# The rotation of the next head's queries: all of it on VectorE, and ahead of both softmax divisions

## The chip, the cores and the metric

One Trainium2 chip, one core of it. The metric is the device time of one execution in microseconds. The engines are called as in the profile: PE (TensorE), DVE (VectorE), ACT (ScalarE), POOL (GpSimd), SP (SyncE, which here issues the DMAs).

## What is computed

One layer of a diffusion backbone over 512 latent and 256 context tokens of width 2048: a modulated RMSNorm, one input projection, then eight heads of gated DeltaNet and eight heads of attention side by side, SiLU gates on both, one output projection and a final RMSNorm. The change lies in the attention heads. There each query head is RMS-normalised, scaled by a weight and rotated by a 2-D axial rotary table, and then meets 768 keys:

```python
def apply_rope(x, cos, sin):
    B, L, H, _ = x.shape
    xr = x.astype(jnp.float32).reshape(B, L, H, 2, 2, ROPE_HALF)
    x1, x2 = xr[..., 0, :], xr[..., 1, :]
    c = cos[None, :, None]
    s = sin[None, :, None]
    out = jnp.stack([x1 * c - x2 * s, x2 * c + x1 * s], axis=-2)
    return out.reshape(B, L, H, HEAD_DIM).astype(x.dtype)
...
def attend(q_blk, k_all, v_all):
    s = jnp.einsum('bqkgd,bskd->bkgqs', q_blk, k_all).astype(jnp.float32) * (HEAD_DIM ** -0.5)
    p = jax.nn.softmax(s, axis=-1).astype(v_all.dtype)
    return jnp.einsum('bkgqs,bskd->bqkgd', p, v_all)
```

## The kernel before, in words

The kernel runs in stages: modulation and norm of the tokens, projections with the DeltaNet scan (up to about 936 us of the span), attention (936 to about 1213 us), output projection with the final norm. Each product is made of three fp32r matmuls from a high and a low half of its operands, so most results are split: ACT writes the rounded high half (L122, L815) and another engine subtracts it to get the low half.

The attention stage is a loop over 17 steps, `for u in range(2 * NH + 1)` (L1266). Step u works on head h = u // 2 and on half qp = u % 2 of its 512 queries (two blocks of 128). Inside this stage the order of the instructions on PE, ACT, DVE and POOL is the order in which the code writes them; each engine runs its own list in that order and waits for what an instruction needs. Four strands are woven together in one step:

- The scores of this step: three matmuls for each part of 128x768 scores into one PSUM tile `s` (`attn_scores`, L1103), the row maxima on DVE (L1114, L1115), the exponentials with their row sums on ACT (L1119, tile `pr`), and for both blocks a reciprocal and a division on DVE (`attn_over`, L1123 to L1125). `pr` holds 128x768 fp32.
- The step before: its divided `pr` blocks are transposed on PE (tile `pt`, L1133), in three groups of 8, split into `pth` on ACT and `ptl` on DVE (L815, L816), and multiplied with the values (tile `o`, `attn_values`, L1140). Two groups of transposes stand at the head of the step ahead of the scores, the third after the first run of filler.
- The filler: the gate projection's matmuls (`fillers`, tile `zl`, L1197), 12 groups of three per step, placed by `fill(n)`: 4 after the scores, 4 before the values, 1 and 3 around the next head's queries. Their weights come by DMA, are split on ACT (L122) and POOL (`wlo_z`, L123). When a projection ends, `z_over` (L1155) puts a tanh on ACT and two operations on DVE (L212, L1161). Every second group also calls for one row of a gate vector: a DMA (`graw`), a scaling on ACT (L1236) and an addition on POOL (`gacc`, L1238).
- The queries of the next head, in odd steps with a head to follow (u = 1, 3, ..., 13, seven of them; they are numbered 1 to 7 here). The generator `attn_norm` (L1075) runs in pieces. Its first piece, in the step before, transposes the raw queries and takes the row sums. The second, called by `next(qns)` after the scores, multiplies by the row's scale on DVE (L1087, the profile gives the helper's line L215: `qn<-qn,hss`) and forms the swapped product on POOL (L1090, `rt<-qn,tabq`; the profile leaves out digits in names, the tile is `rt2`). `swapped` reads each pair of 32 columns in exchanged order. The third piece multiplies by the cosine table (`qn<-qn,tabq`) and adds `rt2` (L1094), both on DVE. It is called between the two calls of `attn_over`. Later in the step `attn_qt` (L1097) transposes the rotated queries on PE (tile `qtp`, L820), and splits them into `qTh` on ACT and `qTl` on DVE (L815, L816). The next step's scores read both.

The transposes of `pt` and `qtp` take turns in two PSUM buffers (tag `t`, `bufs=2`): the second group of `pt` transposes of an even step takes the buffer that `qtp` held until `qTl` was written.

In an odd step the list of DVE after the exponentials is: `ptl` of the third group, reciprocal and division of block 0, the two operations of the rotation, reciprocal and division of block 1, what `z_over` and the values ask for, `qTl`.

Of the kernel before, what the change touches and what calls it, by code (L numbers as in the profile page):

```python
# [68 lines left out]
def build(tc, a):  # L69
    nc = tc.nc  # L70
    V, S, G, T, SY = nc.vector, nc.scalar, nc.gpsimd, nc.tensor, nc.sync
# [134 lines left out]
    def power(x, p):  # L206

        n = x.shape[-1]
        G.tensor_tensor(out=x, in0=x, in1=expo[p][:, :n], op=ALU.pow)

    def silu(eng, out, x, t):
        eng.scalar_tensor_tensor(out=out, in0=t, scalar=1.0, in1=x, op0=ALU.add, op1=ALU.mult)  # L212

    def mul(eng, out, x, y):
        eng.tensor_tensor(out=out, in0=x, in1=y, op=ALU.mult)  # L215
# [570 lines left out]
    def swapped(x):  # L786

        return x.rearrange("p t (a s r) -> p (t a) s r", a=2, s=2)[:, :, ::-1]
# [29 lines left out]
    def transposes(src, t0, n, tp):  # L818
        for t in range(n):
            T.transpose(out=tp[:, t], in_=src[:, (t0 + t) * 128:(t0 + t + 1) * 128], identity=ident)  # L820
        return tp
# [243 lines left out]
    def ttile(shape, nm):  # L1065
        return PSt.tile(shape, F32, tag="t", bufs=2, name=nm)
# [3 lines left out]
    def attn_q(h):  # L1070
        qc = ap_.tile([128, SEQ], F32, tag="qc", bufs=2, name=f"qc{h}")
        SY.dma_start(qc, qad[h])
        return qc

    def attn_norm(h, qc):  # L1075

        tp = transposes(qc, 0, 4, ttile([128, 4, 128], f"qtp{h}"))
        qn = ap_.tile([128, 4, 128], F32, tag="qn", bufs=1, name=f"qn{h}")
        ss = ap_.tile([128, 4], F32, tag="hss", bufs=2, name=f"hss{h}")
        jk = ap_.tile([128, 128], mybir.dt.bfloat16, tag="hjk", bufs=1, name=f"hjk{h}")  # L1080
        S.copy(qn, tp)
        for t in range(4):
            S.activation(jk, qn[:, t], AF.Square, accum_out=ss[:, t:t + 1])
        V.tensor_scalar(out=ss, in0=ss, scalar1=1.0 / 128.0, scalar2=EPS, op0=ALU.mult, op1=ALU.add)
        power(ss, -0.5)
        yield qn
        mul(V, qn, qn, ss.unsqueeze(2).to_broadcast([128, 4, 128]))  # L1087
        t2 = ap_.tile([128, 4, 128], F32, tag="rt2", bufs=1, name=f"rt2{h}")
        tb = A["tab"]
        mul(G, t2.rearrange("p t (a s r) -> p (t a) s r", a=2, s=2), swapped(qn),  # L1090
            tb[:, 1].rearrange("p t (a s r) -> p (t a) s r", a=2, s=2))
        yield qn
        mul(V, qn, qn, tb[:, 0])
        V.tensor_tensor(out=qn, in0=qn, in1=t2, op=ALU.add)  # L1094
        yield qn

    def attn_qt(h, qn):  # L1097
        tp = transposes(qn.rearrange("p t d -> p (t d)"), 0, 4, ttile([128, 4, 128], f"qtp2{h}"))
        qt = [apr.tile([128, SEQ], F32R, tag=i, bufs=2, name=f"{i}{h}") for i in ("qTh", "qTl")]
        split_from(tp.rearrange("p t c -> p (t c)"), *qt)  # L1100
        return qt

    def attn_scores(h, qp, qTh, qTl):  # L1103

        kv = h // 4
        sp = PSs.tile([128, 2 * NTOK], F32, tag="s", name=f"s{h}_{qp}")
        sos = [sp[:, qi * NTOK:(qi + 1) * NTOK] for qi in range(2)]
        mxs = [ap_.tile([128, 2], F32, tag="mx", bufs=4, name=f"mx{h}_{qp}_{qi}") for qi in range(2)]
        for qi in range(2):
            qsl = slice((qp * 2 + qi) * 128, (qp * 2 + qi + 1) * 128)  # L1110
            for c0, c1 in (((0, 512), (512, 768)) if qi == 0 else ((0, 256), (256, 768))):
                mm3(sos[qi][:, c0:c1], qTh[:, qsl], qTl[:, qsl], kTh[:, kv, c0:c1], kTl[:, kv, c0:c1], True, True)
        for qi in range(2):
            V.tensor_reduce(out=mxs[qi][:, 0:1], in_=sos[qi], axis=AX.X, op=ALU.max)  # L1114
            V.tensor_scalar(out=mxs[qi][:, 0:1], in0=mxs[qi][:, 0:1], scalar1=-SC, scalar2=None, op0=ALU.mult)  # L1115
        prs = []
        for qi in range(2):
            pr = ap_.tile([128, NTOK], F32, tag="pr", bufs=4, name=f"pr{h}_{qp}_{qi}")
            S.activation(pr, sos[qi], AF.Exp, bias=mxs[qi][:, 0:1], scale=SC, accum_out=mxs[qi][:, 1:2])  # L1119
            prs.append(pr)  # L1120
        return list(zip(prs, mxs))

    def attn_over(pr, mx):  # L1123
        V.reciprocal(mx[:, 1:2], mx[:, 1:2])
        V.tensor_scalar(out=pr, in0=pr, scalar1=mx[:, 1:2], scalar2=None, op0=ALU.mult)  # L1125

    def attn_pt(h, qp, prs, j2):

        tp3 = ttile([128, 2, 256], f"pt{h}_{qp}_{j2}")
        for qi in range(2):  # L1130
            for jj in range(2):
                j = j2 * 2 + jj
                T.transpose(out=tp3[:, jj, qi * 128:qi * 128 + 128],  # L1133
                            in_=prs[qi][0][:, j * 128:j * 128 + 128], identity=ident)
        pth = ap_.tile([128, 2, 256], F32R, tag="pth", bufs=3, name=f"pth{h}_{qp}_{j2}")
        ptl = ap_.tile([128, 2, 256], F32R, tag="ptl", bufs=3, name=f"ptl{h}_{qp}_{j2}")
        split_from(tp3, pth, ptl)
        return pth, ptl

    def attn_values(h, qp, pts):  # L1140
        kv = h // 4
        op = PSt.tile([128, 256], F32, tag="o", name=f"o{h}_{qp}")
        for j in range(6):
            vsl = slice(kv * 128, kv * 128 + 128)
            mm3(op, vah[:, j, vsl], val[:, j, vsl], pts[j // 2][0][:, j % 2], pts[j // 2][1][:, j % 2], j == 0, j == 5)
        m = M[8 + h][:, qp * 256:qp * 256 + 256]
        if (h, qp) in early:
            V.scalar_tensor_tensor(out=m, in0=m, scalar=0.5, in1=op, op0=ALU.mult, op1=ALU.mult)
        else:
            S.copy(m, op)  # L1150
        done.add((h, qp))
# [107 lines left out]
    def fill(n):  # L1259

        for _ in range(n):
            next(gen, None)
# [3 lines left out]
    for u in range(2 * NH + 1):  # L1266
        h, qp = divmod(u, 2)
        more = h + 1 < NH
        prs, pts = None, []
        if before is not None:  # L1270
            pts = [attn_pt(*before, j2) for j2 in range(2)]
        if h < NH:
            prs = attn_scores(h, qp, *qt)
            if qp == 1 and more:
                next(qns)
            fill(FS + 5 * (before is None))
        if before is not None:
            pts.append(attn_pt(*before, 2))
        if prs is not None:
            attn_over(*prs[0])  # L1280
            if qp == 1 and more:
                qn = next(qns)
            attn_over(*prs[1])
        if before is not None:
            fill(FV)
            attn_values(before[0], before[1], pts)
        if u < NZA:

            e = ap_.tile([128, SEQ], F32, tag="ze", bufs=2, name=f"zae{u}")
            S.activation(e, M[8 + u], AF.Tanh, scale=0.5)  # L1290
            silu(V, M[8 + u], M[8 + u], e)
            early.update(((u, 0), (u, 1)))
        fill(FQ)
        if more:
            if qp == 0:
                qns = attn_norm(h + 1, qcs.pop(h + 1))
                next(qns)
                if h + 3 < NH:
                    qcs[h + 3] = attn_q(h + 3)
            else:  # L1300
                qt = attn_qt(h + 1, qn)
        fill(FR)
        before = h, qp, prs
# [109 lines left out]
```

## Time and profile before

Three runs took 1404.99, 1405.37 and 1408.50 us; the median is 1405.37. The profile was taken from a further execution.

| | |
|---|---|
| time of the profiled execution | 1413.92 us |
| its span, first to last instruction | 1412.1 us |
| PE busy (matmuls) | 1282.5 us, 91% |
| DVE busy | 747.5 us, 53% |
| ACT busy | 608.3 us, 43% |
| POOL busy | 529.4 us, 37% |
| mean granted clock of PE | 0.975 of full speed |

How to read it: busy time is the union of an engine's recorded instructions, and its share is of the whole span, over stages with different limits. A timeline row has the start, the duration, the engine, the line, the operation with its tiles as out<-in, the shape and the count, and in square brackets the idle time of the engine in front of it and what ended that. The granted clock has two levels, full (2.4 GHz, written 1.0) and half (1.2 GHz, 0.5); a mean between them is a stretch with some of each.

### The profile page before, as it was taken

How to read it: one execution, taken by the hardware profiler on the slowest of the kernel's cores; microseconds unless marked ns; L12 is line 12 of the kernel's file. 1: busy time of each engine (PE TensorE's matmuls, PEld its weight loads, DVE VectorE, ACT ScalarE, POOL GpSimd, SP SyncE). 2: the span in 40 equal slices, each digit the busy share in tenths (PEclk: the TensorE clock that was granted, in tenths of full speed). 3: DMA queues.
4: the chain of work that ended last, by engine and by line, in shares of the span. 5: the costliest groups of instructions: out<-in, count | busy, mean ns of one | idle time of the engine just before them, and what ended most of it. 6: DMA issues, size and time to landing. Idle time of an engine off the chain costs nothing.

```text
span 1412.1 us, 24988 instructions
## 1 busy us (share of the span) xinstructions
PE 1282.5 (91%) x9406; PEld 1031.0 (73%) x9406; DVE 747.5 (53%) x1643; ACT 608.3 (43%) x1509; POOL 529.4 (37%) x477
## 2 busy tenths in 40 slices
PE   3788988999999999999999999889889999999997
PEld 1455676877788787787777877667777778787785
DVE  3434685475456656476665524427566655544322
ACT  4111342445444453544545444446556663433221
POOL 1011211334353453443434445435777772012330
PEclk9999998999999999999999999999999999999999
DMA  9999622222322223232232343353545432474202
GB/s 311 255 270 285 180 72 56 71 56 63 67 71 69 66 65 77 58 84 57 81 66 58 84 127 111 93 186 105 145 132 151 134 97 61 164 234 146 90 33 102
DMA packets 264187, 163.52 MB, mean 116 GB/s; under 512 B 63042, under 2 KB 236187, under 8 KB 263043
## 3 DMA queue, kind: packets, MB, share of 16 engines
q1 hardware_dynamic: 264067, 161.93, 41.6%
q8 instruction: 74, 1.21, 0.4%
q14 instruction: 46, 0.38, 0.1%
HBM read 148.33 MB, written 13.56 MB: 115 GB/s over the span
## 4 chain that ended last, share of the span: by engine, by line
PE 55%; DVE 17%; DMA 8%; issue 8%; ACT 7%; POOL 4%; SPq 2%; POOLq 0%; ACTq 0%; DVEq 0%
PE zl L1197 6%; PE vl L157 5%; DMA wada<-in_w_ada 4%; PE kl L157 3%; PE vx L159 3%; DVE cacc_k L199 2%; DVE cacc_v L199 2%; PE kvl L157 2%; PE po L140 2%; PE tsh L751 2%; PE po L141 2%; PE po L139 2%; PE ql L157 2%; PE kx L159 2%; PE tsh L740 2%
## 5 line engine op out<-in xcount | busy, mean ns | idle before, releaser
L215 POOL TENSOR_TENSOR sdh<-sth,egl 128x256 f32<-128x256 f32 x80 | 55.4, 692 | 169.5 <-DVE sth L757 75.8
L1238 POOL TENSOR_TENSOR gacc<-graw,gacc 128x512 f32<-128x512 f32 x60 | 89.3, 1488 | 43.3 <-ACT graw L1236 30.0
L736 ACT ACTIVATE oqh<-ksh,egsw 64x128 f32<-64x128 f32 x128 | 46.3, 362 | 99.0 <-DVE rh L731 98.2
L731 DVE SCALAR_TENSOR_TENSOR rh<-ksh,negeg,vtokh 64x128 f32<-64x128 f32 x176 | 61.1, 347 | 50.8 <-PE ksh L719 47.5
L1197 PE MATMUL zl<-hhL,whi_z 128*128 128x512 f32 x208 | 88.0, 423 | 0.0
L123 POOL TENSOR_TENSOR wlo_z<-wraw_z,whi_z 128x512 fp32r<-128x512 f32 x52 | 70.5, 1358 | 45.0 <-ACT whi_z L122 43.8
L1197 PE MATMUL zl<-hlL,whi_z 128*128 128x512 f32 x208 | 84.9, 408 | 0.0
L1197 PE MATMUL zl<-hhL,wlo_z 128*128 128x512 f32 x208 | 84.8, 408 | 0.1
L140 PE MATMUL po<-wlo_wo,mh 128*128 128x512 f32 x192 | 77.5, 404 | 3.7 <-DVE wlo_wo L123 3.7
L757 DVE TENSOR_TENSOR sth<-sdh,tsh 128x256 f32<-128x256 f32 x80 | 33.7, 421 | 87.1 <-PE tsh L751 81.7
L139 PE MATMUL po<-whi_wo,mh 128*128 128x512 f32 x192 | 76.0, 398 | 1.5 <-ACT whi_wo L122 1.5
L141 PE MATMUL po<-whi_wo,ml 128*128 128x512 f32 x192 | 76.8, 400 | 0.0
L123 DVE TENSOR_TENSOR wlo_wo<-wraw_wo,whi_wo 128x512 fp32r<-128x512 f32 x48 | 37.7, 794 | 66.5 <-ACT whi_wo L122 66.4
L816 DVE TENSOR_TENSOR ptl<-pt,pth 128x512 fp32r<-128x512 f32 x48 | 31.7, 687 | 72.5 <-ACT pth L815 72.4
L1344 POOL TENSOR_TENSOR yx<-yx,tt 128x512 f32<-128x512 f32 x12 | 17.1, 1443 | 126.9 <-DVE tt L215 67.6
L199 DVE SCALAR_TENSOR_TENSOR cacc_v<-craw,cvT,cacc_v 128x512 f32<-128x512 f32 (+1 forms) x64 | 44.0, 734 | 38.8 <-ACT cacc_v L195 38.5
L751 PE MATMUL tsh<-vsh,ktok 128*128 128x128 f32 x352 | 55.6, 281 | 3.6 <-ACT vsh L744 3.2
L323 POOL TENSOR_TENSOR wlo<-wraw,whi 128x384 fp32r<-128x384 f32 x16 | 16.0, 1006 | 110.4 <-ACT whi L322 110.4
L122 ACT CAST whi_wo<-wraw_wo 128x512 fp32r<-128x512 f32 x48 | 29.3, 618 | 61.4 <-PE po L141 37.7
L751 PEld LDWEIGHTS tsh<-vsh,ktok 128*128 128x128 f32 x352 | 47.8, 192 | 10.1 <-ACT vsh L744 4.6
L255 PE MATMUL ada<-wada,cs 128*32 128x256 f32 x512 | 42.3, 417 | 13.9 <-DMA wada<-in_w_ada 13.8
L744 ACT ACTIVATE vsh<-tsh,cch 128x128 f32<-128x128 f32 x88 | 32.2, 366 | 45.9 <-PE tsh L740 44.9
(488 smaller groups left out, 4162.2 us busy)
## 6 DMA issues: line engine op xcount, KB each, us to landing
wada<-in_w_ada SPq DMA_DIRECT2D x128, 256.0 KB, 5.1
graw<-in_w_ada SPq DMA_DIRECT2D x64, 256.0 KB, 2.7
wraw_z<-in_w_in SPq DMA_DIRECT2D x52, 256.0 KB, 3.1
wraw_wo<-in_w_out SPq DMA_DIRECT2D x48, 256.0 KB, 3.1
wraw_q<-in_w_in SPq DMA_DIRECT2D x28, 256.0 KB, 3.2
wraw_k<-in_w_in SPq DMA_DIRECT2D x28, 256.0 KB, 2.8
wraw_v<-in_w_in SPq DMA_DIRECT2D x28, 256.0 KB, 2.8
xs<-in_x SPq DMA_DIRECT2D x4, 1024.0 KB
```

Source lines behind the costliest of these rows:

```text
L123: (lo_eng or G).tensor_tensor(out=lo, in0=raw, in1=hi, op=ALU.subtract)
L139: T.matmul(out, lhsT=lh, rhs=rh, start=start, stop=False, skip_group_check=True)
L140: T.matmul(out, lhsT=lh, rhs=rl, start=False, stop=False, skip_group_check=True)
L141: T.matmul(out, lhsT=ll, rhs=rh, start=False, stop=stop, skip_group_check=True)
L157: T.matmul(pl, lhsT=lw, rhs=rt[0][:, k], start=st, stop=sp, skip_group_check=True)
L159: T.matmul(pc, lhsT=lw, rhs=rt[1][:, k], start=st, stop=sp, skip_group_check=True)
L199: V.scalar_tensor_tensor(out=x, in0=raw[:, i0 + j:i0 + j + m], scalar=w(j), in1=x, op0=ALU.mult, op1=ALU.add)
L215: eng.tensor_tensor(out=out, in0=x, in1=y, op=ALU.mult)
L731: V.scalar_tensor_tensor(out=r[rows], in0=ks[rows, d], scalar=gsc["negeg"][rows, gcol:gcol + 1], in1=vtok[rows, p], op0=ALU.mult, op1=ALU.add)
L751: T.matmul(ts[:, d], lhsT=ktok[:, p, half], rhs=vs, start=True, stop=True, skip_group_check=True)
L1197: T.matmul(pl, lhsT=lw, rhs=rt[:, k], start=st, stop=sp, skip_group_check=True)
L1238: G.tensor_tensor(out=acc, in0=raw, in1=acc, op=ALU.add)
```

## The change

Two edits. The swapped product moves from POOL to DVE, at its old place in the program. The two last operations of the rotation move in front of both divisions; in the list of DVE they now stand after `ptl` of the third group and ahead of the first reciprocal.

```diff
@@ attn_norm
         t2 = ap_.tile([128, 4, 128], F32, tag="rt2", bufs=1, name=f"rt2{h}")
         tb = A["tab"]
-        mul(G, t2.rearrange("p t (a s r) -> p (t a) s r", a=2, s=2), swapped(qn),
+        mul(V, t2.rearrange("p t (a s r) -> p (t a) s r", a=2, s=2), swapped(qn),
             tb[:, 1].rearrange("p t (a s r) -> p (t a) s r", a=2, s=2))
         yield qn
@@ the loop over steps
         if prs is not None:
-            attn_over(*prs[0])
             if qp == 1 and more:
                 qn = next(qns)
+            attn_over(*prs[0])
             attn_over(*prs[1])
```

## Rows read from the trace of the kernel before

**Rows 1.** The waits of PE from 936 to 1210 us: who waited, for whom, us in total, times, the longest.

```profile
PE qtp L820 <- DVE mx L1124: 14.2, 6, 2.7
```

**Rows 2.** The chain of waits from 988 to 1004 us (odd step 2), in order of time: start, us, what.

```profile
992.41 1.72 DVE qn L215
...
994.16 1.66 DVE qn L1094
...
995.97 1.09 PE qtp L820 x4
```

**Rows 3.** Timeline of PE: the transposes of the rotated queries in odd steps 1 to 6, and after the first of them the second group of `pt` transposes of the step that follows.

```profile
962.30 0.63 PE L820 MATMUL qtp<-cmain,qn 128*128 128x128 f32 x4 [1.68 <-DVE mx L1124]
...
965.80 0.66 PE L1133 MATMUL pt<-cmain,pr 128*128 128x128 f32 x4 [0.33 <-DVE qTl L816]
...
995.97 1.09 PE L820 MATMUL qtp<-cmain,qn 128*128 128x128 f32 x4 [2.70 <-DVE mx L1124]
...
1032.79 1.09 PE L820 MATMUL qtp<-cmain,qn 128*128 128x128 f32 x4 [1.78 <-DVE mx L1124]
...
1068.22 0.63 PE L820 MATMUL qtp<-cmain,qn 128*128 128x128 f32 x4 [2.69 <-DVE mx L1124]
...
1101.88 1.09 PE L820 MATMUL qtp<-cmain,qn 128*128 128x128 f32 x4 [2.71 <-DVE mx L1124]
...
1137.27 0.63 PE L820 MATMUL qtp<-cmain,qn 128*128 128x128 f32 x4 [2.62 <-DVE mx L1124]
```

**Rows 4.** Stretches, one for each of the odd steps 1 to 7, from the first transpose of the rotated queries to the first score matmul of the next step: from:to and length in us, busy us of each engine with instructions, then the granted clock, the share of the DMA engines and GB/s.

```profile
962.30:966.22 3.92, 3.58 (x22) 2.89 (x22) 3.66 (x7) 2.62 (x5) 1.34 (x1) 1.00 0.23 62
995.97:1001.92 5.95, 5.95 (x21) 4.97 (x22) 2.41 (x3) 2.61 (x5) 5.84 (x5) 0.53 0.61 171
1032.79:1038.66 5.87, 5.87 (x23) 4.08 (x24) 4.67 (x6) 2.61 (x5) 5.79 (x5) 0.75 0.55 154
1068.22:1071.58 3.36, 3.36 (x22) 2.90 (x22) 2.02 (x2) 2.57 (x5) 2.35 (x3) 1.00 0.57 156
1101.88:1107.79 5.91, 5.91 (x22) 4.93 (x22) 3.67 (x4) 2.61 (x5) 5.42 (x4) 0.53 0.49 139
1137.27:1142.18 4.91, 4.91 (x22) 3.99 (x22) 2.00 (x2) 2.61 (x5) 4.83 (x4) 0.65 0.59 164
1168.17:1172.69 4.52, 4.52 (x23) 2.95 (x24) 3.14 (x5) 1.30 (x3) 1.28 (x1) 1.00 0.18 53
```

**Rows 5.** Timeline of DVE in odd step 2.

```profile
990.96 0.69 DVE L816 TENSOR_TENSOR ptl<-pt,pth 128x512 fp32r<-128x512 f32 x1 [3.10 <-ACT pth L815]
...
991.76 0.65 DVE L1125 TENSOR_SCALAR pr<-pr,mx 128x768 f32<-128x768 f32 x1
992.33 1.79 DVE L215 TENSOR_TENSOR qn<-qn,tabq 128x512 f32<-128x512 f32 x1
994.16 1.66 DVE L1094 TENSOR_TENSOR qn<-qn,rt 128x512 f32<-128x512 f32 x1
...
995.93 1.44 DVE L1125 TENSOR_SCALAR pr<-pr,mx 128x768 f32<-128x768 f32 x1
...
997.71 0.69 DVE L816 TENSOR_TENSOR qTl<-qtp,qTh 128x512 fp32r<-128x512 f32 x1
```

**Rows 6.** Timeline of POOL in odd step 2.

```profile
987.95 1.30 POOL L215 TENSOR_TENSOR rt<-qn,tabq 128x512 f32<-128x512 f32 x1 [0.63 <-DVE qn L215]
989.47 1.29 POOL L1238 TENSOR_TENSOR gacc<-graw,gacc 128x512 f32<-128x512 f32 x1 [0.22 <-ACT graw L1236]
990.73 1.27 POOL L123 TENSOR_TENSOR wlo_z<-wraw_z,whi_z 128x512 fp32r<-128x512 f32 x1
991.95 3.31 POOL L1238 TENSOR_TENSOR gacc<-graw,gacc 128x512 f32<-128x512 f32 x2
```

**Rows 7.** The instructions on tile `qn`, and below them one row of those on the table `tabq`: line, engine, operation, count, duration in ns (least/median/most), first and last start in us, forms. In the row on `tabq` four operations of 128x128 read their second operand swapped, and one of 128x512 reads plainly.

```profile
L215 DVE TENSOR_TENSOR qn<-qn,hss x7: 681/683/1010, 955.4 to 1161.3; 128x512 f32<-128x512 f32 x7
L215 POOL TENSOR_TENSOR rt<-qn,tabq x7: 1297/1304/1312, 956.2 to 1162.0; 128x512 f32<-128x512 f32 x7
L215 DVE TENSOR_TENSOR qn<-qn,tabq x7: 1779/1785/1790, 959.7 to 1165.5; 128x512 f32<-128x512 f32 x7
L1094 DVE TENSOR_TENSOR qn<-qn,rt x7: 691/1640/1670, 961.5 to 1167.3; 128x512 f32<-128x512 f32 x7
...
L215 DVE TENSOR_TENSOR tabq<-tabq,nw x5: 283/284/691, 846.5 to 847.7; 128x128 f32<-128x128 f32 x4, 128x512 f32<-128x512 f32 x1
```

**Rows 8.** Timeline of DVE: `ptl` of the third group in odd steps 1 and 5, with the idle time in front of it.

```profile
958.32 0.69 DVE L816 TENSOR_TENSOR ptl<-pt,pth 128x512 fp32r<-128x512 f32 x1 [2.21 <-ACT pth L815]
...
1096.87 0.69 DVE L816 TENSOR_TENSOR ptl<-pt,pth 128x512 fp32r<-128x512 f32 x1 [3.43 <-ACT pth L815]
```

**Rows 9.** Timeline of DVE: `qTl` in odd steps 1, 3, 4, 5 and 6.

```profile
965.07 0.68 DVE L816 TENSOR_TENSOR qTl<-qtp,qTh 128x512 fp32r<-128x512 f32 x1
...
1036.15 0.68 DVE L816 TENSOR_TENSOR qTl<-qtp,qTh 128x512 fp32r<-128x512 f32 x1
...
1069.56 0.68 DVE L816 TENSOR_TENSOR qTl<-qtp,qTh 128x512 fp32r<-128x512 f32 x1
...
1104.91 0.68 DVE L816 TENSOR_TENSOR qTl<-qtp,qTh 128x512 fp32r<-128x512 f32 x1
...
1138.59 0.68 DVE L816 TENSOR_TENSOR qTl<-qtp,qTh 128x512 fp32r<-128x512 f32 x1
```

## The prediction, made before the changed kernel ran

> **What bounds the kernel now.** I read the waits of PE over the attention stage first, since PE is busy for 91% of the span and a wait of PE there is lost time unless something behind it waits anyway. The reader should see one wait that stands above all: the transposes of the rotated queries wait six times, 14.2 us in total [rows 1]. The row names the reciprocal of L1124, but that is only the next instruction on DVE; the transposes need the addition that ends the rotation. Then the chain of waits: in odd step 2 it runs through the two rotation operations into `qtp`, so this wait sets the end there [rows 2]. Then the single waits: 1.68, 2.70, 1.78, 2.69, 2.71 and 2.62 us in steps 1 to 6; step 7 has none worth a row [rows 3]. Last, the stretches from `qtp` to the next scores: the same work takes 3.36 us at full clock in step 4, and 5.95, 5.91 and 4.91 us in steps 2, 5 and 6, where the granted clock is 0.53, 0.53 and 0.65; with two row sums more it takes 4.52 us in step 7 and 5.87 us in step 3 at 0.75 [rows 4]. So after four of the six waits PE ran at its half level (1.2 GHz) for a while. That costs 2.59 + 2.55 + 1.55 + 1.35 = 8.0 us, on top of the 14.2 us of idle time.
>
> Why is DVE late? In step 2 it writes `ptl`, divides block 0 (0.65 us), multiplies by the cosines (1.79) and adds (1.66); the queries are ready at 994.16 + 1.66 = 995.82, and `qtp` starts 0.15 us later [rows 3, 5]. An operation of that size alone takes 0.68 us [rows 7]. The long ones meet POOL: while the multiplication runs from 992.33, POOL's two `gacc` from 991.95 to 995.26 take 3.31 us where one takes 1.29 [rows 5, 6]. The two engines take turns: each DVE operation that reads two SBUF tiles, and the division of `pr` too, waits about 1.1 us for one POOL operation and then runs.
>
> **The swapped product on DVE.** It stands behind `qn<-qn,hss`, and DVE then waits for `ptl`: 2.21 us in step 1, 3.10 in step 2, 3.43 in step 5 [rows 5, 8]. Its price: 0.68 us if swapped reading costs nothing [rows 7]. Four swapped operations of a quarter of the size took at most 0.284 us each, so four quarters make 1.14 us as an upper bound alone [rows 7]; a wait of 1.1 us for POOL makes 2.2 us. I take 0.7 us: POOL's own `rt` is gone, and its next `gacc` was waiting for ACT (0.22 us of idle time in front of it), so nothing of POOL moves into this place [rows 6]. Both ends lie inside the idle time, the upper one just. The move costs nothing on the path. It takes seven POOL operations of 1.30 us away [rows 7], and for the same reason (the next POOL operation waits for ACT) nothing later on POOL starts earlier. Without that cover it would cost 7 x 0.7 = 4.9 us.
>
> **The rotation ahead of the divisions.** In step 2 `ptl` is done at about 991.6 [rows 5]. The multiplication would start there, while POOL's `wlo_z` is recorded until 992.00 [rows 6]. The division at 991.76 stood in the same place and took 0.65 us, not the 1.44 of a blocked one [rows 5], so POOL lets go of the port near 991.8. I take 0.2 us of waiting and 0.68 of work: 992.5. The waiting `gacc` goes next, and the addition takes 1.66 us as before: ready at 994.2 instead of 995.82, 1.6 us earlier. Bounds: with neither blocked 993.0 (2.8 earlier), with both blocked 995.0 (0.8 earlier). In steps 1 and 7 the addition was unblocked (the 0.69 row in rows 7 stands for two of seven) and only the division is passed: 0.8 us earlier. Applied to rows 3, the waits shrink to 0.9, 1.1, 0.2, 1.1, 1.1 and 1.0 us; 8.8 of 14.2 us go.
>
> By the Trainium skill, "SBUF — State Buffer", Who interferes with whom, whichever of DVE and GpSimd issues first holds the shared port pair for its whole instruction. By that rule the multiplication would wait until 992.00, 0.4 us instead of 0.2, and the saving of a step would be 1.4 us instead of 1.6. The trace agrees on the turns (1.79 against 0.68 us), but the division that took 0.65 us shows the port free before the recorded end.
>
> **What is late next.** The divisions now come after. Before, multiplication, addition and second division were blocked; after, addition, first division and second division. From 994.2: two divisions of 1.44 us, each with about 0.1 us for its reciprocal, end at 997.3; before, the second ended at 995.93 + 1.44 = 997.4 [rows 5]. So the end of DVE's list does not move, and neither does `qTl` at its end, since `qTh` comes earlier. But the next step's second `pt` group needs the buffer that `qTl` frees: in step 1 it already waits for it, 0.33 us [rows 3]. From the end of `qTl` (965.75) to the scores (966.22) it takes 0.47 us [rows 4, 9]. That is the new limit: scores start at the end of `qTl` + 0.47 or when PE gets there, whichever is later. PE gets there 3.36 us after `qtp` (4.52 in steps 3 and 7): in step 2 at 994.35 + 3.36 = 997.7. The limit by `qTl` is later in steps 2 to 6 [rows 5, 9]: 998.87, 1037.30, 1070.71, 1106.06, 1139.74. Against the ends in rows 4 this saves 3.05, 1.36, 0.87, 1.73 and 2.44 us. In step 1 the limit is where it was, and in step 7 PE had no wait: nothing. Sum: 9.45 us, of which 8.0 us is clock given back and 1.4 us idle time. The rest of the wait only changes its place, from `qtp` to `pt`.
>
> **The clock.** So the gain hangs on it. Waits of 2.70, 1.78, 2.71 and 2.62 us came with the half level, 2.69 and 1.68 did not [rows 3, 4]; the size alone doesn't decide. What is left is cut in two with the filler between: 1.1 at `qtp` and 1.2 at `pt` in step 2, 0.2 and 1.6 in step 3, 1.1 and 0.8 in step 4, 1.1 and 2.4 in step 5, 1.0 and 0.7 in step 6. Only step 5 keeps a piece near the old sizes. I expect one short stretch at half level to remain, as in step 6: 4.91 - 3.36 = 1.6 us. Forecast: 9.45 - 1.6 = 7.8 us saved. The steps between are full of PE work and filler, so nothing there should give it back.
>
> On the profiled execution's own time that is 1413.92 - 7.8 = 1406.1 us. The median lies 8.55 us below that execution; I carry the saving over: 1405.37 - 7.8 = 1397.6 us. Its own range is 1395.9 (no half level left) to 1399.4.
>
> **Rivals.**
> - *The half level stays in its places.* PE then needs 5.95, 5.87, 5.91 and 4.91 us from `qtp` on: the savings become 1.6, 1.36, 0.87, 1.6 and 1.6, together 7.0, and some 1.6 us of low clock now falls on scores: 5.4 saved, 1400.0 us. For it: a wait at `qtp` is still there; against it: each is under half as long as it was.
> - *As much half level as before, in front of the scores instead.* Only the idle time is gained, 1.4 us: 1404.0 us.
> - *A fourth blocked operation.* If the multiplication meets the start of a POOL operation rather than its end, it takes 1.79 instead of 0.68 and `qTl` moves 1.1 us back: +1.1, -1.95, -0.26, +0.23, -0.63, -1.34 in steps 1 to 6, 2.85 saved, 1402.5 us. For it: it was blocked in all seven steps [rows 7]; against it: the place it moves to.
> - *Slower: the wait at `pt` brings the half level to every step.* A fall there costs 2.6 us (steps 2 and 5) and falls on scores. Three use up 7.8 of the 9.45 us, from the fourth on the change loses; with six it loses 15.6 - 9.45 = 6.2 us: 1411.5 us. For it: 0.9 to 3.5 us of idle time remains per step, and nearly as much in total as before; against it: it is in pieces.
>
> **How the numbers follow.** Forecast 0.48, half level in place 0.17, half level moved 0.13, fourth blocked operation 0.12, slower 0.10. About 0.3% (4.2 us) is what a measurement of this kernel tells from no change: faster means below 1401.2. The forecast, the second case and a little of the fourth are faster, 0.67; the moved half level, most of the fourth and the mild end of the last are the same, 0.25; slower 0.08. The range goes from 1394.5 (all savings and a kinder clock) to 1404.5; it leaves out the slower case and some of the moved half level.
>
> **What would show it.** DVE has an `rt` of about 0.7 us in the idle time ahead of `ptl`, and POOL none. The multiplication takes 0.7 to 0.9 us in steps 2 to 6 instead of 1.79, the first division 1.44. PE's waits at `qtp` sum to some 5.4 us, and waits of `pt` for `qTl` and the second division of some 7 us appear. The stretches of rows 4 show the clock at 1.0 in most steps. The prediction is wrong if `qTl` ends later than before relative to `ptl`, or if the clock falls as often as now.

## The result, and the profile after

The changed kernel takes 1402.31 us (median of six runs, 1398.76 to 1404.54), the kernel before 1409.0 us (median of six runs, the three known before the prediction among them). The medians differ by 6.7 us. The ratio on record is 0.9939, with a 95% interval of 0.9919 to 0.9959: about 8.6 us less, between 5.8 and 11.4. The forecast was 7.8 us less. In a run of the second edit alone and one of the whole rotation in the idle time, both described below, the mean granted clock was 0.66 and the time 1765 us; medians and ratios leave these two out.

The two profiled executions differ by more, 1412.1 against 1401.1 us of span. One must look where. The attention stage, from its first score matmul to that of the last step, in the kernel before and then in the changed kernel (from:to and length, busy us with instructions for PE, PEld, DVE, ACT and POOL, granted clock, DMA share, GB/s):

```profile
931.23:1186.68 255.45, 233.59 (x1217) 191.27 (x1217) 153.43 (x233) 144.76 (x309) 164.71 (x120) 0.95 0.46 133
```

```profile
926.96:1174.45 247.49, 229.28 (x1216) 187.16 (x1217) 159.55 (x240) 145.19 (x309) 155.85 (x113) 0.98 0.48 138
```

The stage is 255.45 - 247.49 = 7.96 us shorter. The other 3 us lie outside: the first scores start at 926.96 instead of 931.23, 4.3 us earlier, in code that the change doesn't touch, and the part after the stage takes 1.2 us more. So 8.0 us of the 11.0 lie in the stage, which fits the ratio. How much a single execution says is limited, though: the profiled one of the kernel before took 1413.92 us, 4.9 above the median of its six runs, and the first edit alone, which leaves all the waits in place, has a stage of 252.64 us in its trace (below), 5.15 us longer than the changed kernel's. PE's busy time in the stage falls by 4.3 us, its idle time by 3.65.

The waits of PE after the change, as in [rows 1], here from 930 to 1210 us:

```profile
PE qtp L820 <- DVE mx L1124: 5.2, 5, 1.2
PE pt L1133 <- DVE qTl L816: 4.6, 5, 1.9
...
PE gater L1209 <- DVE ze L212: 1.2, 1, 1.2
```

The wait at `qtp` falls from 14.2 to 5.2 us. A wait of `pt` for `qTl` that was there once with 0.33 us now takes 4.6 us in five steps, and the row sum matmul (`gater`) waits 1.2 us in step 3. The single waits on PE's timeline, as in [rows 3], in steps 1, 2, 4, 5 and 6 (step 3 has none):

```profile
956.72 0.63 PE L820 MATMUL qtp<-cmain,qn 128*128 128x128 f32 x4 [0.64 <-DVE mx L1124]
...
990.24 0.63 PE L820 MATMUL qtp<-cmain,qn 128*128 128x128 f32 x4 [1.16 <-DVE mx L1124]
...
1058.14 0.63 PE L820 MATMUL qtp<-cmain,qn 128*128 128x128 f32 x4 [1.13 <-DVE mx L1124]
...
1090.95 0.63 PE L820 MATMUL qtp<-cmain,qn 128*128 128x128 f32 x4 [1.15 <-DVE mx L1124]
...
1126.21 0.63 PE L820 MATMUL qtp<-cmain,qn 128*128 128x128 f32 x4 [1.10 <-DVE mx L1124]
```

And the stretches of [rows 4], from `qtp` to the next scores, for steps 1 to 7:

```profile
956.72:962.18 5.46, 3.58 (x21) 2.88 (x22) 5.39 (x9) 2.83 (x5) 1.27 (x1) 1.00 0.26 62
990.24:994.62 4.38, 3.81 (x21) 2.87 (x22) 3.88 (x5) 2.45 (x4) 4.30 (x4) 1.00 0.56 150
1024.06:1030.27 6.21, 4.97 (x24) 3.33 (x24) 6.12 (x8) 2.70 (x5) 6.13 (x5) 0.94 0.61 169
1058.14:1062.20 4.06, 3.79 (x22) 2.87 (x22) 3.56 (x4) 3.13 (x6) 3.98 (x3) 1.00 0.59 165
1090.95:1096.88 5.93, 3.97 (x21) 3.04 (x22) 5.82 (x7) 3.03 (x6) 5.85 (x5) 0.97 0.42 120
1126.21:1130.28 4.07, 3.80 (x21) 2.86 (x22) 3.57 (x4) 2.34 (x5) 4.07 (x3) 1.00 0.53 141
1155.97:1160.46 4.49, 4.49 (x24) 2.92 (x23) 3.37 (x7) 1.30 (x3) 1.28 (x1) 1.00 0.23 59
```

The granted clock is 1.00 in five of the seven stretches, where it was in three. The idle time is now inside the stretch: in step 2 PE is busy for 3.81 of 4.38 us, in step 5 for 3.97 of 5.93. Not all of the moved wait is recorded as idle time: at clock 1.00 steps 2, 4 and 6 have 3.79 to 3.81 us of busy time where step 4 had 3.36 before, so the sum of wait and stretch is firmer than its split.

DVE in step 2, as in [rows 5]:

```profile
986.78 0.69 DVE L816 TENSOR_TENSOR ptl<-pt,pth 128x512 fp32r<-128x512 f32 x1 [2.24 <-ACT pth L815]
987.39 0.99 DVE L215 TENSOR_TENSOR qn<-qn,tabq 128x512 f32<-128x512 f32 x1
988.42 1.68 DVE L1094 TENSOR_TENSOR qn<-qn,rt 128x512 f32<-128x512 f32 x1
...
990.20 1.46 DVE L1125 TENSOR_SCALAR pr<-pr,mx 128x768 f32<-128x768 f32 x1
...
991.77 1.46 DVE L1125 TENSOR_SCALAR pr<-pr,mx 128x768 f32<-128x768 f32 x1
...
993.48 0.68 DVE L816 TENSOR_TENSOR qTl<-qtp,qTh 128x512 fp32r<-128x512 f32 x1
```

POOL beside it, as in [rows 6]:

```profile
986.55 1.28 POOL L123 TENSOR_TENSOR wlo_z<-wraw_z,whi_z 128x512 fp32r<-128x512 f32 x1
987.79 3.45 POOL L1238 TENSOR_TENSOR gacc<-graw,gacc 128x512 f32<-128x512 f32 x2
```

The swapped product takes 0.69 us in the idle time. The multiplication takes 0.99 us instead of 1.79. Then come three operations of the blocked length: addition 1.68, division 1.46, division 1.46. From the start of `ptl` to that of `qTl` it is 993.48 - 986.78 = 6.70 us; before, 997.71 - 990.96 = 6.75. In all seven steps, as in [rows 7]:

```profile
L215 DVE TENSOR_TENSOR rt<-qn,tabq x7: 691/692/693, 951.3 to 1150.1; 128x512 f32<-128x512 f32 x7
L215 DVE TENSOR_TENSOR qn<-qn,tabq x7: 792/984/1014, 954.1 to 1152.9; 128x512 f32<-128x512 f32 x7
```

### The profile page after: what moved, and what is told of

The parts are those of the page before. It is cut to its first block, busy times and chain, and to the rows that moved or that the text cites. A ratio compares the mean times of both kernels' runs of the same rounds, so it can differ in the third digit from the quotient of the medians.

```text
span 1401.1 us, 24994 instructions
## 1 busy us (share of the span) xinstructions
PE 1277.1 (91%) x9406; PEld 1023.1 (73%) x9406; DVE 755.5 (54%) x1650; ACT 609.2 (43%) x1509; POOL 520.5 (37%) x470
## 4 chain that ended last, share of the span: by engine, by line
PE 53%; DVE 18%; issue 8%; DMA 8%; ACT 7%; POOL 4%; SPq 2%; POOLq 0%; ACTq 0%; DVEq 0%
PE vl L157 5%; PE zl L1197 5%; PE kl L157 3%; PE vx L159 3%; DVE cacc_v L199 2%; DVE cacc_k L199 2%; PE kvl L157 2%; DMA wada<-in_w_ada 2%; PE tsh L751 2%; PE ql L157 2%; PE po L140 2%; PE po L141 2%; PE po L139 2%; PE tsh L740 2%; PE ada L255 2%
## 5 line engine op out<-in xcount | busy, mean ns | idle before, releaser
L1119 ACT ACTIVATE pr<-s,mx 128x768 f32<-128x768 f32 x32 | 28.6, 898 | 53.2 <-PE zl L1197 32.7
```

## The experiments

The first four of the kernels below ran together, the last three together, each beside the kernel before. The stage is always taken as above, from the first scores to those of the last step.

**The first edit alone.**

```diff
-        mul(G, t2.rearrange(...), swapped(qn),
+        mul(V, t2.rearrange(...), swapped(qn),
```

> The first edit alone: the swapped product on VectorE, the rotation's two last operations still between the divisions. Theory (the move is covered by idle time of DVE and takes POOL nothing that anybody waits for): rt takes 0.69 us ahead of ptl, POOL's next gacc still waits for ACT, so the multiplication stays at 1.79 us, PE's waits at qtp stay at about 14 us in six steps with the half level of the clock behind some of them, and the attention stage takes what it took before, within 1 us; ratio 0.998 to 1.002. Rival (POOL's load is what blocks DVE, so 7 x 1.3 us less on POOL gives part of the gain): the multiplication falls well under 1.79 us, the waits at qtp shrink by some 3 us or more, ratio about 0.997.

Measured: ratio 1.0003 (0.9979 to 1.0027). The wait of PE, the multiplication, and then the stage with the stretches of steps 2 and 3:

```profile
PE qtp L820 <- DVE mx L1124: 14.7, 6, 2.7
```

```profile
L215 DVE TENSOR_TENSOR qn<-qn,tabq x7: 1779/1785/1795, 952.1 to 1156.2; 128x512 f32<-128x512 f32 x7
```

```profile
924.77:1177.41 252.64, 230.60 (x1216) 188.80 (x1217) 157.99 (x240) 145.03 (x309) 155.63 (x113) 0.97 0.47 135
988.42:993.32 4.90, 4.90 (x21) 4.07 (x22) 2.34 (x3) 2.61 (x5) 4.82 (x4) 0.65 0.57 161
1024.61:1029.24 4.63, 4.60 (x24) 2.96 (x24) 4.60 (x6) 2.57 (x5) 4.55 (x4) 1.00 0.60 164
```

The multiplication is where it was, 1.785 us in the middle, and the waits at `qtp` sum to 14.7 us. So the swap alone removes nothing that PE waits for, and POOL's seven operations less don't free the port at that place: the theory holds, the rival falls. One part of the expectation missed: the stage of this execution is 2.8 us shorter than before. PE's busy time falls by 3.0 us (233.59 to 230.60) with waits that sum to no less, so it is the clock for the most part. From first scores to next scores, step 2 is 1.08 us shorter (its stretch takes 4.90 us at 0.65, before 5.95 at 0.53) and step 3 is 0.81 us shorter (4.63 us at 1.00, before 5.87 at 0.75, though PE waits 2.65 us in front of it and not 1.78). Another 1.30 us lie in the first step of the stage, 15.82 instead of 17.12 us, where the code is the same; over the nine traces of this document that step takes 15.50 to 17.36 us. The timed runs show none of it, so a single execution can move by that much. The sum that gave 8.0 us of lost clock in the trace before gives 5.8 us in this one (1.54 + 0.11 + 2.60 + 1.55 in steps 2, 3, 5 and 6).

**The second edit alone.**

```diff
-            attn_over(*prs[0])
             if qp == 1 and more:
                 qn = next(qns)
+            attn_over(*prs[0])
             attn_over(*prs[1])
```

> The second edit alone: the rotation ahead of both divisions, the swapped product still on POOL. Theory: rt on POOL ends some 2 us before ptl, so the multiplication doesn't wait for it; steps 2 to 6 look as after the whole change: multiplication about 1.0 us, addition 1.67, both divisions 1.45, waits at qtp about 5 us in all, waits of pt for qTl about 4 to 5 us; the attention stage is 7 to 8 us shorter than before, ratio 0.994. Rival (the edits need each other): the multiplication or the addition waits for POOL's rt, and less than half of the gain is left, ratio 0.997 or more.

Measured: ratio 0.9949 (0.9927 to 0.9972). Waits, the multiplication, stage:

```profile
PE qtp L820 <- DVE mx L1124: 5.2, 5, 1.2
PE pt L1133 <- DVE qTl L816: 4.6, 5, 1.9
```

```profile
L215 DVE TENSOR_TENSOR qn<-qn,tabq x7: 790/977/1001, 957.1 to 1156.4; 128x512 f32<-128x512 f32 x7
```

```profile
930.41:1178.03 247.62, 229.33 (x1217) 187.01 (x1217) 154.32 (x233) 145.20 (x309) 164.84 (x120) 0.98 0.48 138
```

Waits of 5.2 and 4.6 us and a stage of 247.62 us: to 0.2 us what the whole change gives (247.49). So the order is the gain; that the swap adds nothing is shown to within the intervals of the ratios, and it is not needed for the gain.

**The waits filled with work that nobody reads.** The kernel before, with matmuls ahead of the transposes of odd steps 2 to 6. They write a PSUM buffer of tag `t` that nothing reads.

```diff
+                warm = {1: 20, 2: 14, 3: 20, 4: 20, 5: 20}.get(h, 0)
+                if warm:
+                    dmp = ttile([128, 256], f"dmp{h}")
+                for _ in range(warm):
+                    T.matmul(dmp, lhsT=hhL[:, 0, 0:128], rhs=hhL[:, 0, 0:256], start=True, stop=True)
                 qt = attn_qt(h + 1, qn)
```

> The kernel before, with PE's waits of odd steps 2 to 6 filled by matmuls whose results nobody reads: 20 of 128x256 (14 in step 3) ahead of the qtp transposes, about 0.12 us each, 2.3 us (1.6 in step 3) of waits of 2.6 to 2.7 (1.8). DVE's order is that of before, and the queries come no earlier. Theory (8.0 of the change's 9.45 us in its sum is PE's clock, not idle time): no half level after qtp in steps 2 to 6, the stretches from qtp to the next scores take 3.4 us, or up to the limit by qTl + 0.47 (3.0 in step 2 to 4.2 in step 5, 4.5 in step 3), so the attention stage is 7 to 8 us shorter than before without any wait being removed, ratio about 0.994. Rival (idle time is what the change saved, the clock's fall is set by something else): half level as before, stage as before, ratio 0.999 to 1.001.

Measured: ratio 0.9957 (0.9937 to 0.9977). Waits, then the stage and the stretches of steps 2 and 5:

```profile
PE o L139 <- ACT pth L815: 3.5, 4, 1.5
...
PE qtp L820 <- DVE mx L1124: 2.7, 5, 1.5
```

```profile
927.48:1176.68 249.20, 237.48 (x1311) 197.92 (x1311) 153.96 (x233) 144.74 (x309) 164.94 (x120) 0.99 0.48 137
991.47:994.84 3.37, 3.37 (x22) 2.91 (x22) 2.34 (x3) 2.58 (x5) 3.29 (x3) 1.00 0.55 154
1095.18:1099.37 4.19, 3.58 (x22) 2.89 (x22) 4.05 (x5) 3.00 (x5) 4.11 (x3) 1.00 0.36 87
```

No query comes earlier here, and the kernel is faster all the same: the stage is 255.45 - 249.20 = 6.25 us shorter. The stretches of steps 2 and 5 take 3.37 and 4.19 us at clock 1.00; in [rows 4] they took 5.95 and 5.91 at 0.53. The 7 to 8 us expected are not quite reached: a wait of 1.5 us at `o` came up in step 5, and the row for `o` stands at 3.5 us where it is 2.3 in the trace before. The rival falls. The clock alone gives back most of what the change gains (6.25 of 7.96 us in the traces; the timed ratios don't tell the two apart), and with its waits filled PE kept the full clock in the stretches of all six steps, 1 to 6. It is not most of what the waits cost: the next kernel removes them and gains 16.6 us in the trace.

**The whole rotation in the idle time.** After the change, with the multiplication and the addition directly behind the swapped product.

```diff
             if qp == 1 and more:
                 next(qns)
+                qn = next(qns)
             fill(FS + 5 * (before is None))
...
         if prs is not None:
-            if qp == 1 and more:
-                qn = next(qns)
             attn_over(*prs[0])
             attn_over(*prs[1])
```

> The whole rotation in DVE's idle time: after the change, but the multiplication and the addition follow the swapped product at once, ahead of ptl of the third group. Theory (what is left of the change's cost is DVE's list up to qTl, which the rotation lengthens by 1.0 + 1.67 us once ptl is there): queries ready before PE comes for them, waits at qtp nearly 0, qTl 2 to 2.7 us earlier against ptl, waits of pt nearly 0, next scores 3.4 us after qtp in steps 1, 2, 4, 5, 6 and 4.5 in 3 and 7; by the steps of the trace after the change this saves 2.7, 2.2, 1.7, 1.8, 3.7, 1.8 and 0 us, some 13 us more than the change, ratio to before 0.983 to 0.987. Rival 1 (POOL takes turns with the rotation in the idle time and pushes ptl back): ptl 1 us or more later, gain over the change under 6 us. Rival 2 (ACT's and POOL's chain of gate rows or the weight halves become the limit once PE doesn't wait): PE waits for wlo_z or pth instead, gain over the change under 6 us.

Measured: 1392.56 us, ratio 0.988 (0.9846 to 0.9914). Waits of PE, the two operations, and the stage, with the even step that follows odd step 2:

```profile
PE o L139 <- ACT pth L815: 4.1, 5, 1.5
...
PE o L140 <- DVE ptl L816: 2.4, 7, 0.3
```

```profile
L215 DVE TENSOR_TENSOR qn<-qn,tabq x7: 691/691/692, 951.9 to 1141.4; 128x512 f32<-128x512 f32 x7
L1094 DVE TENSOR_TENSOR qn<-qn,rt x7: 691/691/694, 952.7 to 1142.2; 128x512 f32<-128x512 f32 x7
```

```profile
926.20:1165.09 238.89, 227.63 (x1217) 187.49 (x1217) 149.81 (x240) 144.21 (x309) 154.10 (x113) 0.98 0.50 143
990.29:1008.64 18.35, 16.51 (x86) 13.75 (x84) 8.69 (x15) 12.41 (x28) 13.47 (x11) 0.91 0.50 143
```

PE's waits for the rotated queries are gone from the list. Multiplication and addition take 0.691 us in all seven steps: they have the same operands as in [rows 7], where they took 1.785 and 1.640 us, and only their place has changed, so the long durations were waits for POOL and not work. The stage takes 238.89 us, 8.6 less than after the change. The expectation was 13. From first scores to next scores, the odd steps are 15.1 us shorter than after the change, more than was expected of them; the even steps give back 5.8 us and the first step of the stage 0.7. The even step behind step 2 takes 18.35 us where it takes 14.58 in the trace before (1001.92 to 1016.50): the clock is 0.91 in it, and PE waits 1.5 us at `o` for `pth`. So the second rival is right in part: ACT, which splits the third group only behind its weight and gate-row work, became a limit there.

**The same with the swapped product on POOL.**

```diff
-        mul(V, t2.rearrange(...), swapped(qn),
+        mul(G, t2.rearrange(...), swapped(qn),
```

> The whole rotation in the idle time as in e3_first, but the swapped product on POOL: what the first edit is worth where its place is tight. Theory: rt takes 1.30 instead of 0.69 us and hands over twice, so the rotation ends some 0.7 us later than in e3_first, 2.8 us after the first product; in the steps whose idle time was 2.2 us ptl is pushed back by some 0.6 us, and POOL's next gacc meets the addition in the others; PE's wait at o grows in most steps; 1 to 5 us lost against e3_first, ratio to before 0.988 to 0.992. Rival (the cover is long enough for either engine): the stage as in e3_first within 1 us.

Measured beside the two that follow: 1393.6 us, ratio 0.9889 (0.9865 to 0.9912). The wait of PE that grew, the addition, and the stage:

```profile
PE o L140 <- DVE ptl L816: 6.3, 9, 1.0
...
L1094 DVE TENSOR_TENSOR qn<-qn,rt x7: 1653/1670/1673, 951.4 to 1143.0; 128x512 f32<-128x512 f32 x7
```

```profile
925.05:1165.23 240.18, 226.77 (x1217) 186.44 (x1217) 150.72 (x233) 144.51 (x309) 164.86 (x120) 0.99 0.49 142
```

The addition meets POOL in all seven steps (1.67 against 0.69 us), `ptl` comes later, and `o` waits for it 6.3 us instead of 2.4. The stage is 1.3 us longer than with the product on DVE, but the two traces differ by more than that in single steps: step 3 is 3.2 us longer here (its stretch has a clock of 0.72, there 1.00), the even step behind step 2 is 2.1 us shorter. So what of the 1.3 us is the product's is not shown. The timed runs can't tell the two apart either. What is shown of the first edit is 3.9 us less waiting for `ptl` where its place is tight, and no gain that the runs can measure in the change as it was made.

**The third group of transposes earlier.** The kernel with the whole rotation in the idle time, with two filler groups instead of four in front of the third group.

```diff
-            fill(FS + 5 * (before is None))
+            fill(FS + 5 if before is None else 2)
         if before is not None:
             pts.append(attn_pt(*before, 2))
+            if h < NH:
+                fill(FS - 2)
```

> e3_first, and the third group of pt transposes after two of the four filler groups behind the scores instead of after all four, so that its pth stands on ACT ahead of the second half's weight and gate-row work. Theory (what is left in e3_first is ACT's order: five waits of o for pth, 4.1 us, with the 2.4 us for ptl behind them and one fall of the clock): the waits of o for pth fall under 1 us, those for ptl under 2 us, 4 to 8 us less than e3_first, ratio to before 0.982 to 0.985. Rival (ACT is late by its exponentials, or POOL's chain takes the place): waits of o or of zl as large as before, gain over e3_first under 2 us.

Measured: 1392.38 us, ratio 0.9872 (0.985 to 0.9894). Waits and stage:

```profile
PE pt L1133 <- DVE ptl L816: 6.0, 7, 1.9
...
PE o L140 <- DVE ptl L816: 1.2, 2, 0.6
```

```profile
925.84:1164.80 238.96, 225.24 (x1216) 184.24 (x1217) 152.04 (x240) 144.13 (x309) 153.89 (x113) 0.99 0.50 143
```

The waits of `o` for `pth` are gone and those for `ptl` are 1.2 us, as expected, but the stage is as long as without it (238.96 and 238.89 us): now the third group's transposes themselves wait 6.0 us for the `ptl` that frees their PSUM buffer, and `pt` waits 3.0 us for `qTl` where it waited 0.2. This misses the expectation; the rival's second half, that another wait takes the place, is what happened.

**The changed kernel once more.**

> The changed kernel once more, beside the two others of this call. Theory: nothing in it hangs on one profile. Waits at qtp 5 us, waits of pt for qTl 4 to 5 us, multiplication 0.8 to 1.0, addition 1.67 in all seven steps; from the first scores to the last step's 7 to 9 us less than before; ratio 0.992 to 0.996. Rival (the clock's falls of one execution made the difference): more than two falls to the half level between 950 and 1160 us and a stage within 4 us of that before.

Measured: 1402.75 us, ratio 0.9945 (0.9923 to 0.9966). The stage:

```profile
927.37:1175.04 247.67, 229.50 (x1216) 185.63 (x1217) 159.31 (x240) 145.12 (x309) 155.68 (x113) 0.98 0.48 138
```

247.67 us, 0.2 from the first profile. The parts agree less well than the sum. The waits of `pt` for `qTl` are 4.6 us again, but `qtp` waits 6.4 us in six steps (5.2 in five in the first profile), and in step 3 the clock falls:

```profile
1024.06:1031.04 6.98, 6.98 (x23) 4.12 (x24) 6.12 (x8) 2.71 (x5) 6.90 (x5) 0.62 0.56 155
```

That stretch took 6.21 us at 0.94 in the first profile. The whole step is 1.15 us longer, as long as in the kernel before (22.22 and 22.16 us), and the first step of the stage happens to be 1.13 us shorter. The rival falls: there are two falls between 950 and 1160 us, this one and one behind step 5, not more.

## Why the prediction was right, step by step

**Saving and level.** The forecast saving, 7.8 us, lies close to what was measured: 6.7 us by the medians, 8.6 by the ratio, and 7.6 by the medians of the repeat (1402.75 against 1410.32). The forecast time, 1397.6 us, is 4.7 us too low and outside its own narrow range (1395.9 to 1399.4). Of that, 3.6 us is the starting point: 1405.37 was the median of three runs, and with three more it is 1409.0. The price of the clock, 8.0 us, was also read from one execution, 4.9 us above that median; the first edit's trace gives 5.8. That the sum came out so near is in part luck. The time alone would also fit the fourth blocked operation (1402.5 us); the traces rule that out.

**The bound.** That the wait at `qtp` sets the end was right, and so was its cause: with the waits removed the stage is 16.6 us shorter, and the same operations take 0.69 us where POOL leaves them alone.

**The swapped product.** Priced at 0.7 us inside idle time; it takes 0.692 us in all seven steps. Reading the halves in exchanged order costs DVE nothing: the plain product with the cosines takes 0.691 us in the idle time. The upper bound of 1.14 us was far off. That it costs and brings nothing was right, as the first edit alone shows to within its interval (0.9979 to 1.0027).

**The rotation.** Predicted for step 2 were 0.88 us for the multiplication and 1.66 for the addition; measured 0.99 and 1.68. In steps 2 to 6 the multiplication takes 0.95 to 1.01 us, a little above the 0.7 to 0.9 that was named as a sign. The waits at `qtp` were to be 0.9, 1.1, 0.2, 1.1, 1.1 and 1.0 us; they are 0.64, 1.16, none, 1.13, 1.15 and 1.10, together 5.2 against 5.4. The Trainium skill's rule of the port ("SBUF — State Buffer", Who interferes with whom) would have the multiplication wait from 987.39 to the end of `wlo_z` at 987.83, 0.44 us; it waited 0.99 - 0.69 = 0.3. The measurement lies between the rule with the recorded end and the 0.2 us read from the division.

**What is late next.** The step that decides most came out as put: in step 2 the end of DVE's list did not move, 6.70 against 6.75 us from `ptl` to `qTl` (6.35 against 6.33 in step 4, 6.40 against 6.33 in step 6), since three blocked operations stayed three. `pt` waits for `qTl`, and the stretch gets longer by what `qtp` gained. Wait plus stretch, before from rows 3 and 4, after from the rows above, give per step: 5.60 to 6.10, 8.65 to 5.54, 7.65 to 6.21, 6.05 to 5.19, 8.62 to 7.08, 7.53 to 5.17, and 4.52 to 4.49 in step 7. The savings are -0.5, 3.1, 1.4, 0.9, 1.5, 2.4 and 0 us, together 8.8; predicted were 0, 3.05, 1.36, 0.87, 1.73, 2.44 and 0, together 9.45.

Step 1 is the one that was missed. It lost half a microsecond, because a gate product on DVE ahead of `qTl`, which had taken 0.68 us, met POOL. Before and after:

```profile
964.46 0.68 DVE L212 SCALAR_TENSOR_TENSOR M<-zae,M 128x512 f32<-128x512 f32 x1
```

```profile
959.60 1.51 DVE L212 SCALAR_TENSOR_TENSOR M<-zae,M 128x512 f32<-128x512 f32 x1
```

```profile
959.29 1.27 POOL L123 TENSOR_TENSOR wlo_z<-wraw_z,whi_z 128x512 fp32r<-128x512 f32 x1 [3.27 <-ACT whi_z L122]
```

The weight half on POOL starts at 959.29, since the filler ran earlier behind the shorter wait and freed its buffer earlier, and the DVE operation at 959.60 takes 1.51 us. (Before, the weight half started at 964.88, behind the start of the DVE operation.) From the start of `ptl` to that of `qTl` it is 7.56 us where it was 6.75: in this step the prediction's sign of being wrong, a later `qTl`, did appear. In the prediction POOL's later work was taken to stay where it was. Against `ptl` it stayed within 0.2 us in steps 2, 3, 5 and 6, and in step 1, where POOL has no gate rows to add, it came 0.74 us earlier.

**The clock.** One short stretch at half level was to remain, 1.6 us, with step 5 named as the likeliest place. In the step behind step 5, before and after:

```profile
1107.79:1122.22 14.43, 14.43 (x85) 12.37 (x83) 8.13 (x13) 9.34 (x23) 7.27 (x6) 1.00 0.41 115
```

```profile
1096.88:1112.69 15.81, 15.81 (x85) 13.58 (x83) 7.52 (x12) 9.00 (x22) 8.42 (x7) 0.90 0.46 129
```

14.43 us became 15.81, 1.4 us lost, at a clock of 0.90: behind the 1.86 us that `pt` waits in step 5. The repeat and the second edit alone have the same there (15.95 and 15.61 us). So 8.8 - 1.4 = 7.4 us, and about 0.5 us more in the first step of the stage (from its first scores to the second step's 16.63 us instead of 17.12) make the 7.96 us of the stage. That half microsecond is not the change's: it lies well within the 15.50 to 17.36 us that this step takes over the traces. Without it the stage is 7.5 us shorter in the first profile and 6.2 us in the repeat. Step 3 keeps some of the half level too: over the whole step the clock is 0.92 after the change and 0.85 in the repeat, where it was 0.85 before. PE waits 1.49 to 1.79 us at `o` there in all three traces, ahead of `qtp`, and the prediction did not price that wait. One thing in the argument was put too narrowly: of the 9.45 us, 8.0 were put down to the clock and 1.4 to idle time. In the stage PE's busy time fell by 4.3 us and its idle time by 3.65, since the clock in the stage rose from 0.95 to 0.98 and not to 1.0, and since less waiting is recorded behind `qtp` than reckoned: 4.6 + 1.2 us instead of some 7. Against the first edit's trace, which has the old waits, the same split is 1.3 us busy and 3.8 us idle, so how much of the gain is clock depends on the execution.

**The rivals.** The fourth blocked operation did not come: the multiplication took at most 1.01 us. The half level left the stretches of steps 2 and 6, and that of step 5 moved into the even step behind it; in step 3 it was there in the repeat (0.62). It did not come in every step. The filled waits show that the price of the clock, on which most of them rest, is real.

## What to carry to other kernels

Where a strand of work that PE will wait for shares an in-order list with work that is not needed yet, its place in the list decides, and the best place is the idle time ahead of the next outside wait: the change moved the rotation past one division and gained 0.6%, the move past one more wait gained as much again (ratio 0.988). Before counting such a gain, look at what is at the end of the same list: here `qTl` hardly moved, and half of the removed wait came back at the next buffer. And a wait of PE must be priced with the clock behind it, which here cost 8.0 us behind 14.2 us of waits in one trace and 5.8 us behind 14.7 in another; filling the waits with matmuls that nobody reads gave 6 us back without making anything earlier.

## What the runs showed of the hardware

Waits of like size drew the half level in one place and not in another. In the trace before, the 2.69 us of step 4 did not (clock 1.00 behind it) and the 2.70 of step 2 did (0.53); with the first edit alone it was the same (2.69 us and 1.00 in step 4, 2.68 us and 0.65 in step 2). In step 3 the longer wait even kept the clock: 1.78 us with 0.75 behind it before, 2.65 us with 1.00 behind it with the first edit alone. What decides it these runs don't show. The other surprise is how regular the turns of POOL and DVE are: a rotation operation of 0.69 us that arrives as POOL begins took 1.64 to 1.79 us, and one that arrives near the end of POOL's operation 0.79 to 1.01, so the price of a meeting can be read off one row and added up.
